# A hybrid decoder layer on one core: group norm's statistics and x's scaling on other engines, attention's causal corner added by TensorE

## The chip, the core and the metric

The kernel runs on one core of one Trainium2 chip. A core has five engines with queues of their own: TensorE (PE; PEld is its weight load), VectorE (DVE), ScalarE (ACT), GpSimd (POOL) and SyncE (SP), which issues most transfers. They meet through semaphores only. The metric is the device time of one execution in microseconds (us). Three runs of the kernel before took 1525.68, 1518.18 and 1522.67 us: median 1522.67. The profile is of one more run.

## The reference, cut to what matters

```
h = RMSNorm(x, pre_norm_g);  proj = h @ w_in          # x: 1024 x 1024
z, xBC, dt, q, k, v, f, z_att, g_ssm, g_att = split(proj)
xs, B, C = split(silu(causal_conv(xBC)))              # 4 groups, state 128
y = chunked SSD scan(xs, dt, B, C), chunks of 128     # 16 heads of 64
yg = y * silu(z);  per group of 256 channels:
yg = yg * rsqrt(mean(yg * yg) + 1e-6) * ssm_norm_g    # "norm" below
s = q.k / 8 + F[t] - F[s], F = cumsum(log_sigmoid(f)) # 16 heads of 64
s = where(kpos <= qpos, s, -inf);  o = softmax(s) @ v
merged = sigmoid(g_ssm) * (yg @ w_b_ssm) + sigmoid(g_att) * ((o * silu(z_att)) @ w_b_att)
out = x + RMSNorm(merged @ w_out, post_norm_g)
```

All is float32. The kernel keeps the precision by splitting an operand into a high part, rounded to the matmul's format (fp32r), and the rest, and by three passes: high x high, high x low, low x high.

## The kernel before

**Stages.** The prologue loads x in eight tiles of 128 rows, scales each row (`norm_tiles`, L766), turns the tiles on TensorE (`turned`, `pt`) and makes the seven operands of a Strassen-like product (`put`). The second four tiles (`hf == 1`) are scaled by GpSimd (L775). Then the big projection runs as a `Stream` of pairs of 128-column strips. A pair has seven steps; a step is two "halves" of six matmuls of 128x512 (`pb`, `pc`, `pd` are their PSUM banks). Weights come into six `raw` buffers, are split (L200, L201) and evicted by ScalarE and VectorE (L246 to L260). Each `half()` also prepares the operand three steps ahead. There are 504 halves in all.

**Work beside the stream.** Everything else is written as generators that `yield n`: `stream.beside` runs n halves of the stream, then goes on. TensorE's matmuls and turns stay in the order in which the program issues them (`mm`, `turn`); a scheduler orders the other engines. Four groups follow one another: pairs up to x's, then the SSD scan `ssd(g)`, then `gate_and_norm(g)` under the next group's pairs. `gate_and_norm` gates y with `z` from DRAM, squares, sums over 256 channels with a matrix of ones (`pv`), and takes the rows of sums to a column tile by DRAM, because a root of one 1x512 row would use one lane: row to `r_dram`, back as `rc` of 128x8 (column b holds rows of block b), root, reciprocal, written to `rr_dram` element by element, and read again as `r`, broadcast to 128 partitions, for the last multiplication (L713). All five transfers are on GpSimd's queue, in order, and each waits for the one before.

**Attention** takes two heads (64 rows each of the array) at a time, eight head pairs. `scores` makes q.k blocks of 128 queries by up to 512 keys (`unit(i, h)`, 12 of them). GpSimd puts a large value into the corner of `fb` above the diagonal (L918, 64 selects of 128x128 in both heads); VectorE adds `fb` to the scores and finds the minimum `nm` (L927); ScalarE takes the exponential and its sum `sm` (L932). `settle` merges the two halves of the keys, `send` turns the 8 columns of maxima (`tp`), copies them to `st`, writes them to `st_dram` and reads them as rows of `nmr[r]`; `send_sums` does the same for the reciprocal sums. `outputs` makes the blocks again, turned (`sT`), with a fourth pass that subtracts the maximum (`nones` x `nmr[h]`), takes the exponential `pt` (L1018), masks its corner on GpSimd (L1023) and multiplies with v (`av`, one block pair later by `flush`). `done` scales `av` with the gate and the reciprocal sum, loaded there (L1042 to L1047). Eight halves of the stream go beside the scores and ten beside the outputs of each head pair; the eighth has four left beside scores and none beside its outputs, where first products with the branch weights (`ps_in`) start.

**After attention** come the branch products, their gates, the output product (`po`) and the last norm; the change leaves them alone.

## Time and profile before

| What | us |
|---|---|
| median of three runs (1518.18 to 1525.68) | 1522.67 |
| the profiled execution, whole | 1512.78 |
| its span, on which the views rest | 1511.0 |
| TensorE busy / VectorE / ScalarE / GpSimd | 1361.1 / 835.9 / 764.8 / 189.8 |
| first block of attention's scores starts | 716.33 |
| one head pair, scores and outputs, mean of the seven with outputs beside the stream | 65.3 |
| scores of the last head pair start | 1173.69 |

The mean granted clock of TensorE in the profiled execution is 0.957 of full speed. The page gives busy time for each engine, a row of tenths in 40 slices of 37.8 us, the chain of work that ended last, and groups of instructions. A group's line reads: source line, engine, operation, out<-in, shape, count, then busy time, mean ns of one, idle time of the engine just before them and what ended it. An engine's idle time is of interest only where TensorE waits as well.

### The profile page before, as it was taken

Reading aid. Unit: us, or ns where it says so; the run is one execution under the profiler, and the core shown is the slowest. Engines: PE = TensorE matmul, PEld = TensorE weight load, DVE = VectorE, ACT = ScalarE, POOL = GpSimd, SP = SyncE. Lnnn points to the kernel's source line nnn. Section 1 sums busy time; section 2 is a strip of 40 time slices with the busy share of each in tenths; the row PEclk is TensorE's granted clock in tenths of the full one; section 3 lists DMA queues with packets and bytes.
Section 4 is the critical chain, followed back from the end, with each engine's and each line's share of the span. In section 5 each row is a group of like instructions: output and inputs, shape, how many; then the busy total and the mean of one; then the engine's idle time right before and its main releaser. Section 6 shows DMA issues by size and latency. Waiting matters only on the chain.

```text
span 1511.0 us, 19901 instructions
## 1 busy us (share of the span) xinstructions
PE 1361.1 (90%) x6866; PEld 1010.4 (67%) x6866; DVE 835.9 (55%) x1671; ACT 764.8 (51%) x1626; POOL 189.8 (13%) x269
## 2 busy tenths in 40 slices
PE   3899999899889988996899888979899779999998
PEld 2577787677667776775565555656565448888786
DVE  5787857776678568765535435152452523444432
ACT  5645556565556555643657467465665731221221
POOL 2000221021103110410010102111021110000000
PEclk8999999999999999998899999989999789999999
DMA  4032332443344324444441424334232635744432
GB/s 179 30 123 61 131 107 74 136 141 125 72 129 148 112 63 140 149 137 133 147 135 69 161 95 158 104 120 146 85 133 92 202 119 188 227 155 149 145 112 84
DMA packets 109925, 189.58 MB, mean 125 GB/s; under 512 B 11168, under 2 KB 36256, under 8 KB 108800
## 3 DMA queue, kind: packets, MB, share of 16 engines
q1 hardware_dynamic: 105840, 179.15, 36.5%
q0 software_dynamic: 2448, 6.87, 1.7%
q10 hardware_dynamic: 1536, 2.29, 0.4%
q8 instruction: 54, 0.88, 0.2%
q14 instruction: 47, 0.39, 0.1%
HBM read 133.45 MB, written 54.82 MB: 125 GB/s over the span
## 4 chain that ended last, share of the span: by engine, by line
PE 61%; DMA 12%; issue 11%; DVE 7%; ACT 5%; POOL 2%; SPq 2%; POOLq 0%; DVEq 0%; ACTq 0%
PE pb L151 17%; PE ps_in L151 12%; PE pc L151 8%; PE po L151 6%; PE sT L151 5%; PE av L151 4%; PE pd L151 4%; DMA th<-st_dram 3%; PE yps L151 2%; DMA raw<-in_wu 2%; DMA csb<-cs_dram 2%; DMA rr_dram<-rc 1%; ACT sf L932 1%; DMA r<-rr_dram 1%; PE s L151 1%
## 5 line engine op out<-in xcount | busy, mean ns | idle before, releaser
L201 DVE TENSOR_TENSOR wop<-sum,wop 128x512 fp32r<-128x512 f32 x144 | 101.2, 705 | 131.1 <-ACT wop L200 130.6
L1018 ACT ACTIVATE pt<-sT,nfcol 128x512 f32<-128x512 f32 (+1 forms) x192 | 96.3, 580 | 92.8 <-PE sT L151 92.8
L932 ACT ACTIVATE sf<-sf,nm 128x512 f32<-128x512 f32 (+1 forms) x192 | 116.4, 608 | 47.0 <-DVE nm L927 43.4
L927 DVE CUSTOM_DVE_ANT_0 sf<-s,fb 128x512 f32<-128x512 f32 (+1 forms) x192 | 99.5, 553 | 48.6 <-POOL fb L918 25.2
L151 PE MATMUL pb<-x5h,wop 128*128 128x512 f32 x288 | 106.1, 422 | 13.8 <-ACT s L246 13.8
L151 PE MATMUL pd<-x1h,wop 128*128 128x512 f32 x288 | 103.9, 413 | 11.8 <-DVE wop L201 11.8
L200 ACT ACTIVATE wop<-sum 128x512 fp32r<-128x512 f32 x144 | 89.7, 623 | 45.9 <-PE pc L151 27.4
L151 PE MATMUL pb<-x6h,wop 128*128 128x512 f32 x288 | 103.7, 412 | 2.8 <-ACT s L246 2.8
L151 PE MATMUL pc<-x3h,wop 128*128 128x512 f32 x288 | 100.0, 401 | 3.2 <-DVE th L260 3.2
L151 PE MATMUL pc<-x2h,wop 128*128 128x512 f32 x288 | 101.8, 406 | 1.2 <-DVE u L258 0.6
L151 PE MATMUL pb<-x0h,wop 128*128 128x512 f32 x288 | 100.4, 400 | 0.0
L151 PE MATMUL pb<-x4h,wop 128*128 128x512 f32 x288 | 99.3, 399 | 0.1
L201 DVE TENSOR_TENSOR wop<-raw,wop 128x512 fp32r<-128x512 f32 x108 | 75.7, 701 | 40.7 <-ACT wop L200 35.9
L151 PE MATMUL av<-pt,v 128*64 128x512 f32 (+3 forms) x384 | 78.2, 520 | 16.7 <-ACT pt L1018 8.5
L246 ACT ACTIVATE s<-pb 128x512 f32<-128x512 f32 x108 | 63.6, 589 | 57.4 <-PE pb L151 57.0
L200 ACT ACTIVATE wop<-raw 128x512 fp32r<-128x512 f32 x108 | 67.1, 622 | 23.7 <-PE pd L151 16.5
L151 PEld LDWEIGHTS pb<-x5h,wop 128*128 128x128 f32 x288 | 57.2, 199 | 31.3 <-ACT s L246 16.4
L151 PEld LDWEIGHTS pd<-x1h,wop 128*128 128x128 f32 x288 | 55.7, 194 | 31.9 <-DVE wop L201 13.1
L151 PEld LDWEIGHTS pb<-x6h,wop 128*128 128x128 f32 x288 | 55.5, 193 | 20.4 <-ACT s L246 5.2
L151 PEld LDWEIGHTS pc<-x3h,wop 128*128 128x128 f32 x288 | 54.4, 189 | 18.5 <-issue 3.4
L151 PEld LDWEIGHTS pc<-x2h,wop 128*128 128x128 f32 x288 | 55.0, 191 | 17.1 <-issue 4.1
L206 DVE TENSOR_TENSOR sum<-raw 128x512 f32<-128x512 f32 x72 | 52.0, 722 | 25.5 <-DMA raw<-in_wu 25.0
(261 smaller groups left out, 3262.7 us busy)
## 6 DMA issues: line engine op xcount, KB each, us to landing
raw<-in_wu SPq DMA_DIRECT2D x128, 256.0 KB
csb<-cs_dram SPq DMA_DIRECT2D x32, 256.0 KB
fb<-f_dram SPq DMA_DIRECT2D x8, 1024.0 KB
raw<-in_wbs SPq DMA_DIRECT2D x9, 512.0 KB
xt<-in_x SPq DMA_DIRECT2D x8, 512.0 KB
zg_dram<-th SPq DMA_DIRECT2D x16, 256.0 KB
qh_dram<-th SPq DMA_DIRECT2D x16, 256.0 KB
ql_dram<-th SPq DMA_DIRECT2D x16, 256.0 KB
```

The costliest lines, as they stand in the source:

```text
L151: return tc.keep_in_program_order(nc.tensor.matmul(*args, **kw))
L200: nc.scalar.activation(op[:, 0], src, AF.Copy)
L201: nc.vector.tensor_tensor(op[:, 1], src, op[:, 0], ALU.subtract)
L206: nc.vector.tensor_tensor(t, x, y, ALU.add)
L246: nc.scalar.activation(s, ps, AF.Copy)
L927: nc.vector.tensor_tensor_reduce(sf[:, e, 0:w], s[e][:, 0:w], fb[:, e, c0:c1], 1.0, 3.0e38, ALU.add, ALU.min, nm[h][:, e, i : i + 1],)
L932: nc.scalar.activation(sf[:, e, 0:w], sf[:, e, 0:w], AF.Exp, scale=-1.0, bias=nm[h][:, e, i : i + 1], accum_out=sm[h][:, e, i : i + 1],)
L1018: nc.scalar.activation(pt[:, e, 0:w], s[e][:, 0:w], AF.Exp, scale=-1.0, bias=nfcol[:, b, 2 * hp + e : 2 * hp + e + 1],)
```

## The change

TensorE's program grows from 6336 to 6876 instructions: 256 matmuls and as many weight loads for the corner of the scores in bfloat16 (`eye` x `far`, 64 rows), 36 small turns of the norm, and 8 turns fewer in attention. GpSimd's list shrinks from 269 to 179: 64 selects, 4 scalings and 24 transfers go, 2 of setup come. SP issues 12 more transfers.

- **x:** ScalarE scales the second four tiles; the squares' scratch moves to the `th` ring.
- **Norm:** the row of sums is copied to `line`, four turns a half bring it into columns (`pv_t`, `rc`); after root and reciprocal one turn (`pr`) gives eight rows, written with 512 bytes a row and read as `r`, on SP. `z` is loaded two halves ahead into the `csb` ring. L713's successor is kept in program order.
- **Pairs:** z, (b, c), q, x, k, v in a group; the norm no longer waits for the v pair, and the turn of v comes after three halves.
- **Corner:** two passes per head on the diagonal 128 columns add the large value above the diagonal, for the scores alone; the `pt` corner stays on GpSimd.
- **Maxima and sums:** one `nmr` tile holds both halves' rows, `pick[h]` selects; maxima of the upper half are turned a yield later; those of the lower half and the reciprocal sums are turned together (24 columns, `ns`), beside the outputs' second pair of blocks. The gate is loaded and multiplied ahead (`gates`).
- **Halves:** ten before attention instead of eight; five among the score blocks and three after the last (before: seven and one), six beside the outputs; 26 halves in all move ahead of attention. The first branch weights load in another order.

```diff
@@ -678,40 +678,54 @@
             sl = half(ch)
             sq = []
             for j in range(2):
-                z = small()
+                z = sp.tile([P, 4, P], F32, tag="csb", bufs=2, name="z").rearrange("p a b -> p (a b)")
                 nc.sync.dma_start(z, zg_dram[2 * g + j, :, sl])
+                sq.append(z)
+            yield 2
+            for j in range(2):
+                z = sq[j]
                 nc.vector.tensor_tensor(xs[j][:, sl], xs[j][:, sl], z, ALU.mult)
                 nc.scalar.activation(z, xs[j][:, sl], AF.Square)
-                sq.append(z)
             nc.vector.tensor_tensor(sq[0], sq[0], sq[1], ALU.add)
...
             yield 6
             pv = pp.tile([P, HALF], F32, tag="tr", bufs=2, name="pv")
             for j in range(2):
                 mm(pv, onesr, sqp[j], start=(j == 0), stop=(j == 1))
-            row = sp.tile([P, 4, P], F32, tag="ce", bufs=1, name="row").rearrange("p a b -> p (a b)")[0:1, :]
-            nc.scalar.activation(row, pv[0:1, :], AF.Identity, bias=eps4[0:1, :], scale=1.0 / 256.0)
-            nc.gpsimd.dma_start(r_dram[g : g + 1, sl], row)
-        rc = sp.tile([P, NT], F32, tag="rc", bufs=1, name="rc")
-        nc.gpsimd.dma_start(rc, r_dram[g].rearrange("(b p) -> p b", p=P))
-        yield 5
-        nc.scalar.activation(rc, rc, AF.Sqrt)
+            line = sp.tile([P, 4, P], F32, tag="ce", bufs=1, name="line")[0:1]
+            nc.scalar.activation(line, pv[0:1, :].rearrange("p (a b) -> p a b", a=4), AF.Copy)
+            yield 2
+            pc = pp.tile([P, HALF], F32, tag="tr", bufs=2, name="pv_t")
+            for b in range(4):
+                turn(pc[:, b : b + 1], line[:, b, :], ident[0:1, 0:1])
+            if ch == 0:
+                rc = sp.tile([P, NT], F32, tag="rc", bufs=1, name="rc")
+            nc.vector.tensor_copy(rc[:, 4 * ch : 4 * ch + 4], pc[:, 0:4])
+        nc.scalar.activation(rc, rc, AF.Sqrt, bias=eps4, scale=1.0 / 256.0)
         nc.vector.reciprocal(rc, rc)
-        nc.gpsimd.dma_start(rr_dram[g].rearrange("(b p) -> p b", p=P), rc)
+        yield 3
+        pr = pp.tile([P, HALF], F32, tag="tr", bufs=2, name="pr")
+        turn(pr[0:NT, 0:P], rc)
+        row = sp.tile([P, 4, P], F32, tag="ce", bufs=1, name="row")[0:NT, 0, :]
+        nc.scalar.activation(row, pr[0:NT, 0:P], AF.Copy)
+        nc.sync.dma_start(rr_dram[g].rearrange("(b p) -> b p", p=P), row)
         r = [sp.tile([P, 4, P], F32, tag="csb", bufs=2, name="r").rearrange("p a b -> p (a b)") for _ in range(2)]
         for ch in range(2):
-            nc.gpsimd.dma_start(r[ch], rr_dram[g : g + 1, half(ch)].to_broadcast([P, HALF]))
+            nc.sync.dma_start(r[ch], rr_dram[g : g + 1, half(ch)].to_broadcast([P, HALF]))
         yield 5
         for ch in range(2):
...
+                tc.keep_in_program_order(
+                    nc.vector.scalar_tensor_tensor(
+                        xs[j][:, sl], xs[j][:, sl], ng[:, i : i + 1], r[ch], ALU.mult, ALU.mult
+                    )
                 )
                 nc.sync.dma_start(ys_dram[i, :, sl], xs[j][:, sl])
...
     def groups_pairs(g):
         return [
+            both("z", g, lambda i: silu_gate(zg_dram, i)),
             Pair((("b", g), ("c", g)), (conv(g, "bt", 8 + g), conv(g, "ct", 12 + g))),
-            both("z", g, lambda i: silu_gate(zg_dram, i)),
+            both("q", g, lambda i: parts(qh_dram, ql_dram, i, -0.125)),
             Pair((("x", 2 * g), ("x", 2 * g + 1)), tuple(conv(g, f"xs{j}", 2 * g + j) for j in range(2))),
-            both("q", g, lambda i: parts(qh_dram, ql_dram, i, -0.125)),
             both("k", g, lambda i: parts(kh_dram, kl_dram, i, 1.0)),
             both("v", g, values),
         ]
...
-    order[0:4] = [order[n] for n in (1, 3, 0, 2)]
+    order[0:4] = [order[n] for n in (0, 2, 1, 3)]
...
-                sqt = wp.tile([P, HALF], F32, tag="s", bufs=3, name="sqt").bitcast(BF16)
+                sqt = small("sqt").bitcast(BF16)
                 nc.scalar.activation(sqt, xt, AF.Square, accum_out=ss[:, t : t + 1])
...
                 if hf == 0:
                     nc.vector.tensor_scalar(xt, xt, rstd[:, t : t + 1], None, ALU.mult)
                 else:
-                    nc.gpsimd.tensor_scalar(xt, xt, rstd[:, t : t + 1], None, ALU.mult)
+                    nc.scalar.activation(xt, xt, AF.Copy, scale=rstd[:, t : t + 1])
...
             stream.beside(norm)
-            stream.until(by_group[g][2])
+            stream.until(by_group[g][3])
             stream.halves(7)
             stream.beside(ssd(g))
-            stream.until(order[6] if g == 0 else by_group[g][5])
             norm = gate_and_norm(g)
...
+        nmr = ap.tile([P, HALF], F32R, name="nmr")
+        pick = [ap.tile([P, 1], F32R, name=f"pick{h}") for h in range(2)]
+        eye = ap.tile([P, 192], BF16, name="eye")
+        far = ap.tile([P, 192], BF16, name="far")
+        nc.vector.memset(eye, 0.0)
+        for t in (nmr, *pick):
+            nc.vector.memset(t.bitcast(F32), 0.0)
+        big, beyond = small("big"), small("beyond")
+        nc.vector.memset(big[:, 0:192], -NEG)
+        for e in range(2):
+            for h in range(2):
+                nc.vector.memset(pick[h][64 * e + 32 * h : 64 * e + 32 * h + 1, :].bitcast(F32), -1.0)
+            nc.vector.tensor_copy(eye[rows[e], 64:P], ident[rows[e], rows[e]])
+            nc.gpsimd.affine_select(
+                beyond[:, 192 * e : 192 * e + 192], big[:, 0:192], [[1, 192]], ALU.is_gt, 0.0, base=64 * e - 64,
+                channel_multiplier=-1,
+            )
+            nc.vector.tensor_copy(far[rows[e], :], beyond[rows[e], 192 * e : 192 * e + 192])
+        corner = [(eye[:, 64:192], far[:, 64:192]), (eye[:, 0:P], far[:, 0:P])]
...
+        def to_rows(cols, n):
             tp = pp.tile([P, HALF], F32, tag="s", bufs=4, name="tp")
             turn(tp[0:n, 0:P], cols)
-            st = ap.tile([16, P], F32, tag="st", bufs=2, name="st")
+            st = ap.tile([24, P], F32, tag="st", bufs=1, name="st")
             nc.scalar.activation(st[0:n, :], tp[0:n, 0:P], AF.Copy)
...
+            return st
...
+        def keep_maxima(hp, r, st):
+            nc.sync.dma_start(st_dram[hp, 0:2, half(r)].rearrange("e (i p) -> e i p", p=P), st)
+        def send_maxima(hp, r):
+            for e in range(2):
+                row = nmr[64 * e + 32 * r : 64 * e + 32 * r + 1, :]
+                nc.sync.dma_start(row.bitcast(F32), st_dram[hp, e : e + 1, half(r)])
...
+        def passes(s, w, ops, corner_at=None):
+            for m, (x, y) in enumerate(ops):
+                for e in range(2):
+                    mm(
+                        s[e][:, 0:w], x[rows[e]], y[rows[e]], start=(m == 0),
+                        stop=(m == len(ops) - 1 and corner_at is None), skip_group_check=True,
+                    )
+            if corner_at is not None:
+                for n, (x, y) in enumerate(corner):
+                    for e in range(2):
+                        mm(
+                            s[e][:, corner_at : corner_at + P], x[rows[e]], y[rows[e]], start=False, stop=(n == 1),
+                            skip_group_check=True,
+                        )
+        def blocks(name):
+            return [pp.tile([P, HALF], F32, tag="s", bufs=4, name=name) for e in range(2)]
...
+            nr1 = ap.tile([P, 2, 4], F32R, tag="nr1", bufs=2, name="nr1")
+            ns = ap.tile([P, 24], F32R, tag="ns", bufs=2, name="ns")
+            nr = [ns[:, 0:8].rearrange("p (e i) -> p e i", e=2), nr1]
+            inv = ns[:, 8:24].rearrange("p (e i) -> p e i", e=2)
...
-                if h == i // 4:
-                    gsl = slice(i * P, (i + 1) * P)
-                    nc.gpsimd.affine_select(
-                        fb[:, :, gsl], fb[:, :, gsl], [[0, 2], [-1, P]], ALU.is_ge, -NEG, base=0, channel_multiplier=1
-                    )
...
+                s = blocks("s")
+                ops = [(q[x][:, isl], k[y][:, 0:w]) for x, y in (("qh", "kh"), ("qh", "kl"), ("ql", "kh"))]
+                passes(s, w, ops, w - P if h == i // 4 else None)
...
+            def finish():
                 nc.vector.tensor_scalar(sm[0], sm[0], 2.0, None, ALU.mult)
-                nc.vector.reciprocal(sm[0], sm[0])
...
+                nc.vector.reciprocal(inv.bitcast(F32), sm[0])
+            def send():
+                st = to_rows(ns.bitcast(F32), 24)
+                keep_maxima(hp, 0, st[0:8, :])
+                nc.sync.dma_start(st_dram[hp, 2:4, :].rearrange("e (i p) -> e i p", p=P), st[8:24, :])
...
             unit(7, 0)
             unit(6, 0)
-            yield 2
+            yield 1
             unit(5, 0)
             unit(4, 0)
             settle(1)
-            yield 2
+            yield 1
             unit(3, 0)
             unit(2, 0)
-            send(1)
             yield 1
+            keep_maxima(hp, 1, to_rows(nr1.bitcast(F32).rearrange("p e i -> p (e i)"), 8)[0:8, :])
+            send_maxima(hp, 1)
             unit(1, 0)
             unit(0, 0)
             settle(0)
-            sums()
-            waiting.append(lambda: send(0))
-            yield 1
-            flush()
-            waiting.append(send_sums)
+            finish()
+            sends.append(send)
+            yield 3
+        sends = []
         def outputs(hp, qk, v, more):
+            zr = {}
+            def gates(h):
+                sl = half(h)
+                zr[h] = ap.tile([P, HALF], F32, tag="zr", bufs=1, name="zr")
+                nc.sync.dma_start(zr[h], za_dram[hp, :, sl])
+                rb = small()
+                for e in range(2):
+                    nc.sync.dma_start(rb[rows[e], :], st_dram[hp, 2 + e : 3 + e, sl].to_broadcast([64, HALF]))
+                nc.gpsimd.tensor_tensor(zr[h], zr[h], rb, ALU.mult)
...
+                    s = blocks("sT")
+                    ops = [(k[x][:, bsl], q[y][:, o:]) for x, y in (("kh", "qh"), ("kl", "qh"), ("kh", "ql"))]
+                    passes(s, w, ops + [(pick[h].to_broadcast([P, P]), nmr[:, o:])])
...
                 def done(h=h, av=av):
-                    sl = half(h)
...
-                for b in range(0, last + 1, 2):
+                    with tc.high_priority():
+                        nc.vector.tensor_tensor(zr[h], av[0], zr[h], ALU.mult)
+                    nc.sync.dma_start(ya_dram[hp, :, half(h)], zr[h])
+                for n, b in enumerate(range(0, last + 1, 2)):
                     flush()
+                    if (h, n) == (1, 1):
+                        sends.pop()()
                     waiting.append(unit(b))
                     waiting.append(unit(b + 1))
+                    if (h, n) in ((1, 2), (0, 0)):
+                        gates(h)
                     if b + 2 > last:
                         waiting.append(done)
                         more(h)
-                    yield 1 if b < 4 * h else 2
+                        if h:
+                            send_maxima(hp, 0)
+                    yield (1, 1, 0, 2)[n] if h else 1
...
-        stream.halves(8)
+        stream.halves(10)
...
-            ws = [load_split(a["wbs"][i], [P, NK, P]) for i in range(2)]
...
+        ws = [load_split(a["wbs"][0], [P, NK, P])]
+        next(go)
+        ws.append(load_split(a["wbs"][1], [P, NK, P]))
         products = first_products()
         for n, _ in enumerate(outputs(hp, [qk[hp, 0], qk[hp, 1]], v, more)):
-            for _ in range((3, 1, 1, 1, 1, 1)[n]):
+            for _ in range((2, 1, 1, 1, 1, 1)[n]):
                 next(go, None)
-            if n:
+            if n > 1:
                 next(products)
```

## The prediction

> **What bounds the kernel now.** I read the page first, then TensorE's waits, then windows of 25 us, and last the timelines of the places where a window is thin.
>
> ```profile
> span 1511.0 us, 19901 instructions
> ...
> PE 1361.1 (90%) x6866; PEld 1010.4 (67%) x6866; DVE 835.9 (55%) x1671; ACT 764.8 (51%) x1626; POOL 189.8 (13%) x269
> ...
> PE   3899999899889988996899888979899779999998
> ...
> PEclk8999999999999999998899999989999789999999
> ...
> PE 61%; DMA 12%; issue 11%; DVE 7%; ACT 5%; POOL 2%; SPq 2%; POOLq 0%; DVEq 0%; ACTq 0%
> ```
>
> TensorE is busy 90% of the span and no other engine over 55%. So time can come only from the 150 us in which it is idle, and from stretches in which its clock digit is under 9. The waits say who leaves it idle (total us, times, longest):
>
> ```profile
> PE tp L154 <- DVE sm L965: 19.7, 8, 3.1
> PE pb L151 <- ACT s L246: 16.6, 9, 6.9
> PE pt L154 <- POOL xt L775: 14.5, 4, 7.5
> PE s L151 <- DVE nm L927: 12.7, 25, 3.4
> PE pd L151 <- DVE wop L201: 11.8, 3, 5.6
> ...
> PE tp L154 <- DVE nm L927: 9.0, 8, 1.7
> ...
> PE tp L154 <- DVE nr L944: 7.8, 8, 3.3
> ```
>
> The three `tp` lines (36.5 us) are attention's turned sums and maxima, `pt` the second half of x, `pb` and `pd` weights or evictions late behind the group norm. The windows (length, PE, PEld, DVE, ACT and POOL busy, granted clock, DMA share, GB/s) place them:
>
> ```profile
> 25.00:50.00 25.00, 10.95 (x44) 5.44 (x45) 11.90 (x23) 12.40 (x24) 11.67 (x4) 0.66 0.10 32
> ...
> 250.00:275.00 25.00, 19.41 (x79) 15.46 (x78) 14.38 (x26) 10.35 (x21) 2.02 (x3) 0.86 0.40 112
> ...
> 700.00:725.00 25.00, 12.60 (x36) 7.99 (x34) 11.11 (x20) 4.05 (x8) 1.52 (x3) 0.73 0.78 269
> ...
> 1175.00:1200.00 25.00, 17.60 (x96) 11.36 (x94) 17.96 (x63) 21.38 (x61) 5.08 (x8) 0.81 0.57 190
> 1200.00:1225.00 25.00, 14.57 (x56) 7.71 (x58) 10.08 (x10) 12.04 (x18) 3.33 (x2) 0.70 0.65 201
> ```
>
> A thin window also has a granted clock under 1.00: a wait is paid for again in slow matmuls after it (12 matmuls of 512 columns, a step of the stream, take 2.75 us at full clock). The norm's chain shows among the transfers (KB, median us from issue to landing):
>
> ```profile
> r<-rr_dram POOLq DMA_DIRECT2D x8, 256.0 KB, 4.2
> ...
> r_dram<-row POOLq DMA_DIRECT2D x8, 2.0 KB, 1.8
> ...
> rc<-r_dram POOLq DMA_DIRECT2D x4, 4.0 KB, 3.5
> rr_dram<-rc POOLq DMA_DIRECT2D x4, 4.0 KB, 10.2
> ```
>
> Writing 4 KB as 1024 pieces of 4 bytes takes 10.2 us.
>
> **Part 1, ScalarE scales x.** GpSimd scales four tiles in 11.67 us (28.74 to 40.4, 2.9 each); TensorE waits 7.46 + 3 x 2.35 = 14.5 us for them. A 128x1024 pass takes ScalarE 1.05 us, so four cost 4.2. `sqt` also moves to another ring, and the instruction order now puts the squares ahead of and between the first operands' copies, where ScalarE idles some 8 us between 10.9 and 25; x has landed by then. ScalarE's last operand copy before the second half's rows ends at 27.5 now; without its squares and roots (4 x 1.5) and with four scalings it would end at 29 at most, against 40.5. I take -11; if the scalings queue behind everything, 4.5 is added to 27.5 and -8 is left; with the slow clock (0.66) gone too, -13.
>
> **Part 2, norm at three inner boundaries.** At group 0, the row goes out at 242.85, `rc` comes back, the write of `rr_dram` runs 250.3 to 260.3, `r` lands at 265.2; VectorE idles 8.36 us for it, with the next weight split behind it on its queue, and TensorE 5.59 (then 1.43 and 1.31). Against the typical pace of the stream the three boundaries lose 6.5, 8.3 and 9.0 = 24 us. Now the columns come by eight turns, the root is taken on 128x8, one turn gives eight rows of 512 bytes: `r_dram` and `rc` go, the write has the 1.7 us of attention's `st_dram` write, the read stays at 4.2 to 4.9. From the reciprocal: 3 halves (4.1 us), the turn, 0.3 copy, 1.7 + 4.9 us, with 5 halves (6.9 us) of cover: VectorE comes to `xs` about when `r` lands. The write, and both reads, move from GpSimd's queue to SP's, where they wait for ScalarE's `row` ahead of later weight loads; those have six buffers, so a wait under one step costs nothing, and over it, itself. Added on TensorE: 9 small turns a group, 0.5 us, 2 in all. I leave 4 us of stalls: -18 (bounds -10, the write and its waits late; -24, all gone).
>
> That the reads join the loads is weighed by one more rule. The Trainium skill, "DMA: Bandwidth & Descriptors", section "Issuing engines are not separate DMA queues", says that transfers from all issuing engines end on the same 16 DMA engines. By it the read gains nothing from the other queue; the sum has nothing for it either.
>
> The pairs' new order, `z` loaded two halves before its use (into `csb`), and `v` turned a half later move work under the same stream and add no operation: 0. Their cover is the stream; without it a 256 KB load is 4.2 us per half group.
>
> **Part 3, last boundary and attention's start.** There TensorE idles 6.86 at 707.83 (weights late behind the scattered write) and 3.21 at 716.33 (first `qh`), and runs at half clock until 744. From `pv` at 684.2 to the first score 14 halves (19.4 us) take 32.1: 12.7 lost. The first scores phase takes 35.66 against 22.3 for the same work without a gap or slow clock: 13.4 lost, with VectorE waiting 8.25 for GpSimd's mask on `fb`, whose load was issued at 715.46. Now ten halves instead of eight stand between loads and scores, the mask is gone, and the write is short. Of 26 us I take 15 (bounds 8 and 22): the load of `fb` (1 MB) still shares the stretch with `r`.
>
> **Part 4, attention.** Head pairs 1 to 6 take 64.7 us; clean, scores are 22.3 (8 halves) and outputs 32.5 (10). Above that the phases lose 39 (scores 1 to 6), 21 (outputs 0 to 6), 12 (last scores) and 17 (last outputs and what follows): 89. Four halves per head pair move ahead of attention: the same 5.5 us elsewhere, 0, but cover that is gone here. Terms after:
>
> - corner on TensorE: 64 diagonal blocks x 2 passes x 2 heads = 256 matmuls of 128 columns. Eight such take 0.42 us in the 128-wide score blocks (pairs of heads side by side), with weight loads of 64x128 (0.185 each) hidden: 0.105 a pair, 13. No bf16 pair is in the trace; bounds 7 (half of the row of 256 columns, 0.11) and 256 x 0.185 = 47, every load exposed. I take 13, since the nearest row hides the same loads.
>
> The Trainium skill speaks against the corner: "TensorE: Matmul & The Clock Gate", section "LDWEIGHTS (loading the stationary operand)", says a load costs by its 128 columns, however few rows it has (107 ns by its formula). By that the corner would be an estimated 27 us and the sum 14 worse; the 128-wide score blocks already run faster than it.
>
> - new waits: the turned maxima are now sent behind a half and the sums with row 0 in one turn, three halves after the last block, which takes out the `tp` waits. In return the units (7,0) and (5,0) have one half behind them instead of two, `av` of blocks 4 and 5 follows its `sT` with no half between (exp 0.52 + select + latency, about 1.5), row 0 of `nmr` is read on SP behind four 256 KB loads of the next `qk` (1.5 past two halves), row 1 0.5, scores 1.5: about 5 per head pair with slow clock, 40 in all (bounds 16 and 76).
> - the tail: the split of `ys` starts only after the last half; ten 512 KB loads through two buffers take about 5.8 us a pair, under outputs with 12 score blocks as cover: 20 lost against 17 + 12 before's last phases (bounds 10 and 30).
>
> 13 + 40 + 20 = 73 against 89: -16. With every bound together -50 and +64; with two of three at their bad ends, +20 to +35.
>
> **The sum.** -11 - 18 - 15 - 16 = -60. The profiled run took 1512.8 (span 1511.0), so 1452.8; the median shown is 9.9 above it, and I predict in its terms: 1463.
>
> **Rivals.**
> 1. Attention's waits only change places. For it: outputs already waits 8.2 for `th` L1047 and 8.5 for `pt`; against: 36.5 us of `tp` waits have no successor of their size. Attention +8 instead of -16, boundaries -6 instead of -18: -24, 1499.
> 2. More comes out: few new waits (attention -40 and each other term near its good end): -90, 1433. For it: boundary losses repeat at each group with one cause.
> 3. Slower: ScalarE and VectorE pace the scores when the cover is thin. Place: blocks (7,0) to (0,0). The last head pair, with four halves, shows it: 28.5 us for work of 16.8, ScalarE busy 21.38 of 25, VectorE 17.96, TensorE 17.60. At that pace plus one half (1.4), then three halves (4.1) and the corner (1.6), scores take 35.6 against 28.8 on average: +6.8, x 8 = 54. Outputs keep their loss. -11 - 18 - 5 + 54 = +20: 1543. It decides from +4.3 us per scores phase (34 / 8), above 33. Against: 25.2 us of VectorE's idle time ahead of those blocks was GpSimd's masks.
> 4. Corner's weight loads exposed: 47 instead of 13: -26, 1497. That the norm's chain isn't shortened would need the 512-byte write to cost as the 4-byte one: +18, 1481, inside the range.
>
> **How the numbers follow.** Forecast 0.50 (own range 1440 to 1485), rival 1 0.18, rival 2 0.15, rival 3 0.12, rival 4 0.05. A change below 0.5% (7.6 us) can't be told from none here. Rivals 1 and 4 reach into "same" with a fifth of their chance; rival 3 is slower with 0.10 and same with 0.02: faster 0.84, same 0.06, slower 0.10. Leaving out the far ends of rivals 2 and 3, the range is 1425 to 1510.
>
> **What would show it.** Right: POOL gone from `pt`'s releasers and window 25:50 above 18 busy; no idle VectorE over 3 us before `xs`; `tp` waits under 10 us; no slow clock in 725:750. Wrong: `rr_dram` or `nmr` landing after 5 us; scores phases over 33 us; `av` or `sT` waiting for `pt` or `nmr` more than 2 us each head pair; corner matmuls spaced over 0.15 us a pair.

## The result and the profile after

The changed kernel takes 1420.72 us (median of four runs, 1416.50 to 1424.67) against 1520.70 (four runs, 1518.18 to 1525.68): 6.6% faster, ratio 0.9338 with a 95% interval of 0.9300 to 0.9377. That is 100 us, where 60 were forecast; the time lies 4 us below the range of 1425 to 1510. The direction and the kind of gain were right, the sizes too small.

The page of the changed kernel (busy time, tenths in 40 slices of 35.4 us, granted clock in tenths, chain of waits):

```profile
span 1414.8 us, 20283 instructions
...
PE 1343.9 (95%) x7150; PEld 1002.7 (71%) x7150; DVE 830.1 (59%) x1689; ACT 763.5 (54%) x1626; POOL 133.7 (9%) x179
...
PE   6899999999999999999999999999999799999998
...
PEclk9999999999999999999999999999999999999999
...
PE 75%; ACT 9%; DMA 7%; DVE 5%; issue 2%; SPq 1%; POOL 0%; DVEq 0%; ACTq 0%; POOLq 0%
```

TensorE is busy 95% of the span, and no slice has a clock digit under 9; the mean granted clock went from 0.957 to 0.991. In the clock's record, stretches at half speed add up to 131.3 us before and 27.0 after. DMA's share of the chain fell from 12% to 7%, GpSimd's from 2% to 0.

TensorE's waits after (us in total, times, longest):

```profile
PE av L151 <- POOL pt L1074: 14.9, 9, 3.0
PE pb L151 <- ACT s L246: 12.5, 9, 2.7
...
PE s L151 <- ACT st L921: 5.5, 8, 1.2
PE s L151 <- DVE nm L979: 3.2, 4, 2.3
PE av L151 <- ACT pt L1069: 3.1, 2, 2.1
...
PE sT L151 <- DMA nmr<-st_dram: 1.4, 4, 0.5
```

The three `tp` waits (36.5 us) are gone, as are GpSimd's four for `pt` in the prologue (14.5) and `pd` behind the norm (11.8). New are `av` behind GpSimd's mask on the probabilities, 5.5 us for the copy `st`, and little for `nmr` (1.4). The windows at the old thin places (length, busy PE, PEld, DVE, ACT, POOL, granted clock, DMA share, GB/s):

```profile
25.00:50.00 25.00, 22.97 (x103) 11.93 (x101) 23.53 (x39) 18.61 (x31) 0.00 (x0) 1.00 0.13 43
...
250.00:275.00 25.00, 22.40 (x91) 17.74 (x91) 21.72 (x35) 15.68 (x31) 1.27 (x1) 0.93 0.50 140
...
700.00:725.00 25.00, 21.76 (x131) 14.40 (x129) 17.11 (x54) 17.30 (x47) 0.00 (x0) 0.93 0.49 184
...
1125.00:1150.00 25.00, 20.55 (x104) 14.15 (x104) 9.27 (x8) 12.47 (x21) 4.79 (x8) 0.80 0.62 204
```

The prologue's window went from 10.95 to 22.97 busy. The window that still has a clock of 0.80 is the start of the branch products beside the last outputs.

Where the 96 us of the two profiled executions (1511.0 and 1414.8) come from can be read by milestones: the start of a certain matmul in both traces, with the stream's halves issued until then counted at 1.375 us each, so that halves moved across a milestone cancel. ("Saved" is the difference so corrected, "step" its growth from one milestone to the next.)

| Milestone on TensorE | before (halves) | after (halves) | saved | step |
|---|---|---|---|---|
| first `df` (prologue) | 41.72 (4) | 27.74 (4) | 14.0 | 14.0 |
| first scan, group 0 | 163.27 (69) | 150.29 (69) | 13.0 | -1.0 |
| first scan, group 1 | 309.46 (153) | 309.80 (167) | 18.9 | 5.9 |
| first scan, group 2 | 459.18 (237) | 449.63 (251) | 28.8 | 9.9 |
| first scan, group 3 | 609.33 (321) | 591.34 (335) | 37.2 | 8.4 |
| first score | 716.33 (374) | 702.80 (400) | 49.3 | 12.0 |
| first `ps_in` (end of attention) | 1213.39 (504) | 1120.88 (504) | 92.5 | 43.2 |
| end | 1504.09 (504) | 1408.04 (504) | 96.0 | 3.5 |

### The profile page after: what moved, and what is told of

Read it like the earlier page. It is cut to its first block, busy times and chain, and to the rows that moved or that the text cites. A ratio compares the mean times of both kernels' runs of the same rounds, so it can differ in the third digit from the quotient of the medians.

```text
span 1414.8 us, 20283 instructions
## 1 busy us (share of the span) xinstructions
PE 1343.9 (95%) x7150; PEld 1002.7 (71%) x7150; DVE 830.1 (59%) x1689; ACT 763.5 (54%) x1626; POOL 133.7 (9%) x179
## 4 chain that ended last, share of the span: by engine, by line
PE 75%; ACT 9%; DMA 7%; DVE 5%; issue 2%; SPq 1%; POOL 0%; DVEq 0%; ACTq 0%; POOLq 0%
PE pb L151 21%; PE ps_in L151 12%; PE pc L151 12%; PE po L151 6%; PE pd L151 6%; PE sT L151 5%; PE av L151 4%; ACT sf L984 4%; DMA csb<-cs_dram 2%; PE yps L151 2%; PE s L151 1%; DVE sf L979 1%; DMA nmr<-st_dram 1%; PE st L151 1%; ACT wop L200 1%
## 5 line engine op out<-in xcount | busy, mean ns | idle before, releaser
L979 DVE CUSTOM_DVE_ANT_0 sf<-s,fb 128x512 f32<-128x512 f32 (+1 forms) x192 | 97.2, 553 | 28.7 <-PE s L151 9.8
L620 POOL TENSOR_TENSOR ce<-ce,ct 128x512 f32<-128x512 f32 x28 | 37.9, 1352 | 368.0 <-ACT ce L619 245.2
L607 ACT ACTIVATE m<-csb,cscol 128x128 f32<-128x128 f32 x128 | 41.3, 391 | 48.0 <-DMA csb<-cs_dram 25.1
```

The lines of the kernel that those rows point to most:

```text
L607: nc.scalar.activation(m4[:, h, :], csb[:, h, :], AF.Relu, scale=-1.0, bias=cscol[:, c, 4 * g + h : 4 * g + h + 1])
L620: nc.gpsimd.tensor_tensor(ce, ce, ct[:, cs].unsqueeze(1).to_broadcast([P, 4, P]), ALU.mult)
L979: nc.vector.tensor_tensor_reduce(sf[:, e, 0:w], s[e][:, 0:w], fb[:, e, c0:c1], 1.0, 3.0e38, ALU.add, ALU.min, nm[h][:, e, i : i + 1],)
```

## The experiments

Each of the first ten undoes one part of the changed kernel, or two, or doubles one. "Slower" is against the changed kernel's median, 1420.7; the kernel before took 1517.8 to 1519.5 us beside these sets, 1520.7 beside the changed kernel. The runs of one kernel spread over 3 to 13 us (8 for the changed kernel), so differences of 2 or 3 us can't be told from none. The parts, undone, add up to most of the gain: the squares' ring 14.5, the norm's way 38, mask and sends together 36, of 100.

**x by GpSimd again.**

```diff
-                    nc.scalar.activation(xt, xt, AF.Copy, scale=rstd[:, t : t + 1])
+                    nc.gpsimd.tensor_scalar(xt, xt, rstd[:, t : t + 1], None, ALU.mult)
```

> The changed kernel with one line undone: GpSimd scales the second four tiles of x again; the squares keep their new ring. The prologue gained 13 us. Theory 1, the engine that scales is the cause: GpSimd's 11.7 us for four tiles stand alone again and the kernel is about 13 us slower than the changed one (1434). Theory 2, the squares' new ring is half of it, since the roots are ready some 10 us earlier and GpSimd starts at about 19 instead of 28.7: only 4 to 6 us slower (1426).

1425.95 (1424.83 to 1430.94), 5 us slower, which is theory 2 by the time; but the first `df` comes at 28.48, only 0.7 us later, and the rest is not placed. So the other half was tried by itself.

**The squares back in the old ring.**

```diff
-                sqt = small("sqt").bitcast(BF16)
+                sqt = wp.tile([P, HALF], F32, tag="s", bufs=3, name="sqt").bitcast(BF16)
```

> The changed kernel with ScalarE scaling x but the squares' scratch back in the ring of three that the stream's evictions use. With GpSimd scaling and the new ring the first df came only 0.7 us later. Theory 1, the ring is what moved the squares ahead: the first df comes 6 to 10 us later than in the changed kernel (at 34 to 38 instead of 27.7) and the kernel is 6 to 10 us slower. Theory 2, either of the two alone suffices: under 2 us.

1435.18 (1433.61 to 1436.88), 14.5 us slower, first `df` at 37.17 (9.4 later): theory 1 by the place, 4.5 us beyond it by the time. ScalarE's timeline of this kernel, the first square of the second four tiles (start, us, instruction):

```profile
25.29 1.05 ACT L783 ACTIVATE sqt<-xt 128x1024 bf16<-128x1024 f32 x1
```

and of the changed kernel, the first and last square of the second four tiles:

```profile
11.45 1.06 ACT L783 ACTIVATE sqt<-xt 128x1024 bf16<-128x1024 f32 x1 [0.47 <-DMA xt<-in_x]
...
17.70 1.04 ACT L783 ACTIVATE sqt<-xt 128x1024 bf16<-128x1024 f32 x1
```

The squares' scratch shared three buffers with the stream's evictions and so stood behind them in turn; in the other ring the squares run 14 us earlier. With the new ring GpSimd's 11.9 us of scaling start at 13.4 instead of 28.7 and fit under the first halves too. The scaling by ScalarE, which the change names, gives 4.6 us of the prologue's 14 where the ring is old (41.72 to 37.17), and 0.7 where it is new.

**The norm by DRAM, all of it, and the scattered write alone.** First the old chain (row to `r_dram`, `rc`, root, `rr_dram`, on GpSimd's queue; its lines stand in the diff above), then only its write:

```diff
-        pr = pp.tile([P, HALF], F32, tag="tr", bufs=2, name="pr")
-        turn(pr[0:NT, 0:P], rc)
-        row = sp.tile([P, 4, P], F32, tag="ce", bufs=1, name="row")[0:NT, 0, :]
-        nc.scalar.activation(row, pr[0:NT, 0:P], AF.Copy)
-        nc.sync.dma_start(rr_dram[g].rearrange("(b p) -> b p", p=P), row)
+        nc.sync.dma_start(rr_dram[g].rearrange("(b p) -> p b", p=P), rc)
```

> The changed kernel with the norm's old way through DRAM (r_dram, rc, rr_dram element by element, all on GpSimd's queue); pair order, early z and the removed stop before the norm stay. From the first scan to the first score the change gained 36 us. Theory 1, the chain of five transfers is the cause: 25 to 36 us slower than the changed kernel (1446 to 1457). Theory 2, the pairs' new order and the missing stop give the cover: at most 10 us slower (1430).

> The changed kernel in which the reciprocals go to DRAM straight from the column tile, in pieces of 4 bytes, on SP; the turn of the rows, its copy and the 512-byte write go. The first step of the chain (columns by turns) stays. The old chain cost 42 us over the four boundaries. Theory 1, the scattered write is most of it, 10 us against under 2: 6 to 9 us at each boundary, 25 to 35 slower (1446 to 1456). Theory 2, the number of transfers on one queue is: 1 to 3 us a boundary, under 12 slower.

The whole chain: 1458.65 (1456.45 to 1460.46), 38 us slower, 9.3, 11.2, 10.9 and 12.3 at the four boundaries. The write alone: 1456.72 (1455.09 to 1459.41), 36 us slower, with 5.8, 10.1, 8.7 and 9.2 there. Theory 1 in both, 1 to 2 us beyond its range. SP's queue at the first boundary of the kernel with the scattered write, and of the changed kernel:

```profile
242.21 0.38 SPq L712 DMA_DIRECT2D rr_dram<-rc  x1
251.40 3.13 SPq L715 DMA_DIRECT2D r<-rr_dram  x2
```

```profile
243.49 0.34 SPq L716 DMA_DIRECT2D rr_dram<-row  x1
244.71 0.82 SPq L719 DMA_DIRECT2D r<-rr_dram  x2
```

The read goes out when the write has landed: 9.2 us after it in pieces of 4 bytes, 1.2 us in rows of 512 (9.1 to 12.4 and 1.2 to 1.3 over the four boundaries). The scattered write costs the same on SP's queue as the whole old chain on GpSimd's, so it is not the queue. One turn on TensorE is worth nearly all of the norm's part; the first step (columns by turns instead of `r_dram` and `rc`) adds 2 us, inside the scatter.

**The old pair order and stop.** (z second, q fourth, `stream.until` the v pair before the norm.)

> The changed kernel with the old order of a group's pairs and the old stop, by which the norm waits until the v pair is through. Theory 1, order and stop move work alone: within 4 us. Theory 2, they give the norm's chain another pair's steps to run under, so that its end meets the convolutions of the next group: 8 to 15 us slower over the four boundaries.

1418.11 (1415.34 to 1419.28): 3 us faster, not told from none. Theory 1; by itself the reordering is worth nothing that these runs can tell.

**The mask, the sends, and both.** The mask back on GpSimd (`affine_select` on `fb`, no corner), then the sends and the scores' cover at their old places, then both:

```diff
             unit(6, 0)
-            yield 1
+            yield 2
...
-            yield 1
+            yield 2
             unit(3, 0)
             unit(2, 0)
-            yield 1
             keep_maxima(hp, 1, to_rows(nr1.bitcast(F32).rearrange("p e i -> p (e i)"), 8)[0:8, :])
             send_maxima(hp, 1)
+            yield 1
...
-            sends.append(send)
-            yield 3
...
+            waiting.append(send)
+            yield 1
+            flush()
...
```

> The changed kernel with the corner undone: GpSimd writes the large values into fb again, TensorE adds no corner. Theory 1, the masks made the waits of attention and the corner is a good trade: 13 us of TensorE come back and 20 to 35 us of waits return, so 5 to 20 us slower (1426 to 1440). Theory 2, attention gained by the later sends alone: the corner is pure cost and the kernel is 10 to 13 us faster (1409).

> The changed kernel with the old places of the sends and of the cover in the scores: maxima of the upper half turned right after blocks (3,0) and (2,0), sums and the other maxima one half after the last block, and the halves among the blocks 1, 1, 2, 2, 0, 1 and 1 at the end. Theory 1, the later sends are what attention gained: TensorE waits again for the turned sums, 2 to 3 us and more in each head pair with the slow clock behind it, 20 to 30 us slower than the changed kernel (1441 to 1451). Theory 2, GpSimd's masks were the root of those waits: without them VectorE is on time, at most 6 us slower, and perhaps faster, since two halves again cover the blocks (7,0) to (4,0).

> The changed kernel with both the mask back on GpSimd and the sends at their old places. Alone the mask cost 12 us by the runs and the early sends 11. Theory 1, the two add up: 20 to 26 us slower than the changed kernel (1441 to 1447). Theory 2, they make one chain (mask, VectorE's minimum, reciprocal, turn), whose idle time is long enough to halve the clock behind it: 33 to 45 us slower (1454 to 1466), with over 40 us of slow clock in attention, as before the change.

1433.54 (1428.27 to 1434.32), 13 slower; 1431.95 (1431.26 to 1436.24), 11 slower; both 1457.16 (1456.09 to 1458.95), 36 slower. The mask alone is theory 1, the sends alone lie between their theories, and both together cost 12 more than their sum: theory 2 of the third run, with 47.8 us at half clock between the first score and the first `ps_in`. TensorE's timeline at the turn of the sums, head pair 2 (start, us, instruction, idle before), with both, and with the early sends alone:

```profile
859.39 0.28 PE L154 MATMUL tp<-ident,ns 128*24 128x128 f32 x1 [3.41 <-DVE ns L1012]
```

```profile
847.11 0.27 PE L154 MATMUL tp<-ident,ns 128*24 128x128 f32 x1 [1.29 <-DVE ns L1007]
```

and windows of the kernel with both, around it:

```profile
850.00:860.00 10.00, 5.15 (x30) 3.55 (x32) 7.16 (x27) 6.77 (x22) 1.61 (x3) 1.00 0.58 205
860.00:866.00 6.00, 6.00 (x28) 3.61 (x26) 0.00 (x0) 2.53 (x4) 0.73 (x2) 0.72 0.24 74
```

VectorE, late by GpSimd's masks, is late with the reciprocal: TensorE waits 3.41 us instead of 1.29, and behind that the clock falls (0.72 in the window after it). With both, each of the first seven outputs phases has 3.41 us at half clock; with either alone none of them has any. The longer wait itself makes up the excess, though: a scores phase (head pairs 1 to 5) takes 27.5 us with both, 25.3 with the early sends alone, 24.3 with the mask alone and 24.5 with neither. The outputs phases (head pairs 1 to 6) take 30.6 with both, slow clock included, and 30.8 with the mask alone, where `sT` waits up to 1.6 us for `nmr`. TensorE's wait of 3.41 us has the length of a stretch of slow clock by chance: the seventh such wait was 2.88 us and had 3.41 at half clock behind it too.

**The corner twice.**

```diff
-                for n, (x, y) in enumerate(corner):
+                for n, (x, y) in enumerate(corner + corner):
...
```

> The changed kernel with the corner's two passes made twice (512 matmuls instead of 256; the masked value is doubled). Theory 1, a pair of corner matmuls takes 0.105 us as in the 128-wide score blocks: 13 us slower (1434). Theory 2, each weight load of 128 columns counts: 27 us (0.107 each) to 47 us (0.185 each) slower. Theory 3, it fills waits of TensorE for VectorE: under 6 us slower.

1425.21 (1423.86 to 1430.25), 4.5 us slower; a scores phase grows from 24.5 to 24.74. The timeline of the changed kernel's TensorE, a block's corner and the next block:

```profile
815.38 0.29 PE L151 MATMUL s<-far,eye 64*128 64x128 bf16 x4
815.48 0.42 PE L151 MATMUL s<-kh,qh 64*128 64x384 f32 x2
```

Four corner matmuls take 0.10 us from start to the next start, and where they are doubled four more take 0.11: 0.05 to 0.06 a pair, half of the value taken, 6.4 to 7.2 us for the 128 pairs. The kernel with the mask on GpSimd agrees: there TensorE's scores phase, less its idle time, is 0.79 us shorter, 6.3 in eight. Doubling hides partly in waits (idle time of a scores phase 0.77 to 0.57). Theory 3 holds by its time.

**The gate late.** (`gates(h)` at the head of `done` again.)

> The changed kernel with the gate and the reciprocal sums loaded and multiplied at the end of each outputs phase again, not ahead. Theory 1, the next phase's first av waits for that product again as before (8.2 us in 4 waits): 8 to 15 us slower (1429 to 1436). Theory 2, the early sums are enough and the loads land under the last blocks: within 4 us.

1422.75 (1422.28 to 1428.44), 2 us slower: theory 2.

**Tries at a faster kernel.** The cover of the upper half's outputs spread evenly, then with its empty place at blocks without a mask:

```diff
-                    yield (1, 1, 0, 2)[n] if h else 1
+                    yield 1
```

```diff
-                    yield (1, 1, 0, 2)[n] if h else 1
+                    yield (1, 0, 1, 2)[n] if h else 1
```

> A try at a faster kernel: in the outputs of the upper half one half of the stream after each two blocks (1, 1, 1, 1) in place of 1, 1, 0, 2. In the changed kernel av waits 14.9 us for the masked pt, 1.25 to 3.0 a time, where no half lies between. Theory 1, that wait goes and nothing takes its place: 6 to 9 us faster than the changed kernel (1412 to 1415). Theory 2, row 0 of the maxima then lands late for the next sT (two halves lay over its read): the wait moves there, within 3 us.

> The changed kernel with the cover in the upper half's outputs as 1, 0, 1, 2: the two blocks without a half behind them are (2) and (3), whose pt has no mask, and the two halves over the read of row 0 stay. Even cover (1, 1, 1, 1) had been 19 us slower. Theory 1, that loss was the read of the maxima (two halves are needed there) and av's wait is for GpSimd's mask: 5 to 9 us faster than the changed kernel (1412 to 1416). Theory 2, av waits for ScalarE's exponential as long as for the mask, or GpSimd's product of the gate comes to lie before the mask: within 3 us, or up to 10 slower.

1439.33 (1436.77 to 1450.11), 19 us slower, and 1420.90 (1415.49 to 1424.57), the same. Waits of the first:

```profile
PE av L151 <- POOL pt L1074: 14.2, 8, 3.1
...
PE sT L151 <- DMA nmr<-st_dram: 11.4, 7, 2.0
```

and of the second:

```profile
PE av L151 <- POOL pt L1074: 6.3, 3, 2.4
...
PE sT L151 <- DMA nmr<-st_dram: 3.5, 5, 1.4
```

Evenly spread, the wait for row 0 of the maxima grows from 1.4 to 11.4 us while the mask's stays: theory 2, but six times its price. Slow clock makes up most of the rest. The seven outputs phases beside the stream are 16.5 us longer in all; TensorE is idle in them 8.5 us more, and four of them have about 3.4 us at half clock, where the changed kernel has none. The clock changes only on a grid of 3.41 us, and what counts is how much idle time falls into one window of it. Windows of the even cover's kernel around two waits for row 0, of 1.66 us (ended at 817.03) and of 1.67 us (ended at 872.58):

```profile
814.17:817.59 3.42, 1.76 (x17) 1.11 (x15) 1.98 (x3) 0.66 (x2) 0.00 (x0) 1.00 0.91 301
817.59:821.00 3.41, 3.41 (x14) 2.58 (x11) 0.00 (x0) 2.21 (x4) 0.81 (x2) 0.50 0.27 77
868.79:872.20 3.41, 2.12 (x16) 0.97 (x14) 1.98 (x3) 1.11 (x2) 0.41 (x1) 1.00 0.90 303
872.20:875.61 3.41, 3.03 (x18) 2.23 (x20) 0.00 (x0) 2.21 (x4) 0.41 (x1) 1.00 0.38 133
```

The first wait lies in one window, and the next window has half clock; the second is cut in two (1.29 and 0.38 us), and nothing follows. The last section has the count over all traces.

In the second try (theory 2) the mask's wait falls by 8.6 us, and the time stays: idle time of the seven outputs phases fell from 1.3 to 2.3 each to 0 to 1.7 (6 us in all), but the phases are less than 1 us shorter in all. Why is not shown.

Then `r` in the ring `th`, alone, with the old pairs, and with the moved cover:

```diff
-        r = [sp.tile([P, 4, P], F32, tag="csb", bufs=2, name="r").rearrange("p a b -> p (a b)") for _ in range(2)]
+        r = [small("r") for _ in range(2)]
```

> A try at a faster kernel: the two broadcast tiles r of the norm go to the ring th instead of csb. In the changed kernel the next scan's first csb load waits for r to be used, ScalarE stands at it, and TensorE waits 12.5 us for evictions behind that. Theory 1, the ring is that wait: 5 to 8 us faster (1413 to 1416). Theory 2, th (four buffers) is short then and the stream's own results wait for it: 0 to 10 us slower.

> A try at a faster kernel: old pair order and stop (1418.1 alone) with r in the ring th (1419.0 alone). Theory 1, the two small gains are real and add up: 3 to 6 us faster than the changed kernel (1415 to 1418). Theory 2, both are scatter between runs: within 3 us.

> All three of the above together. Theory 1: 10 to 14 us faster than the changed kernel (1407 to 1411). Theory 2: no faster than the changed kernel.

1418.99 (1411.13 to 1423.67) alone, not told from none; 1411.74 (1409.83 to 1414.33) with the old pairs, 9 us faster and beyond theory 1; 1414.21 (1410.23 to 1416.38) with all three, 6.5 us faster, between its theories. In the middle one each of the six runs lies under the changed kernel's four; its ratio to the kernel before is 0.9311 (0.9277 to 0.9344), whose interval overlaps the changed kernel's, and the kernel before was 3 us faster beside it. Its wait for evictions shows where the gain may come from:

```profile
PE pb L151 <- ACT s L246: 2.4, 4, 0.7
```

It was 12.5 in the changed kernel: there the next scan's `csb` load waits until `r` is used, ScalarE waits for `csb`, and evictions stand behind it. With the ring alone it is 4.4, with the old pairs alone 9.0. So the ring takes most of this wait, and the 3.41 us of slow clock behind it at two boundaries; why its time falls only with the old pairs was not tried.

## Why the prediction came out as it did

| Term | forecast | measured | by |
|---|---|---|---|
| prologue | -11 | -13.0 | milestones |
| three inner boundaries | -18 | -24.3 | milestones |
| last boundary and first scores | -15 | -12.0 - 7.3 = -19.3 | milestones; first scores 35.66 to 28.35 |
| attention and tail | -16 | -43.2 + 7.3 - 3.5 = -39.4 | milestones, less the first scores |
| pair order | 0 | 0 | old order, 3 us faster |

**The step that failed is the size of the attention term's new waits**: "about 5 per head pair with slow clock, 40 in all". Counted as the prediction counts, by how far the phases lie above their clean lengths, they cost 25: the scores of head pairs 1 to 6 lie 13.3 above, outputs 0 to 6 with six halves 16.6, less 4.8 for the corner. The mechanism (late sends remove the `tp` waits, others come in return) was right; three of the four waits hardly came. `av` behind `pt`, put at 1.5 a head pair, is 1.2 to 2.2 in the first seven, as said (9.7 of its 18.0; the rest falls after the last outputs start). But rows 0 and 1 of `nmr`, put at 1.5 and 0.5, cost 1.4 in all, and the blocks (7,0) and (5,0), put at 1.5, wait for VectorE in the first scores phase alone (3.2). `st`, 0.6 a phase, wasn't foreseen. Idle time in these 13 phases is 15.8 us; the other 9 are not placed.

The four waits add up to 5.0 a head pair by themselves, so the words "with slow clock" had no figure in the sum. Slow clock did not come either: from the wait before the first score to the first `ps_in` half speed takes 71.7 us before and only 3.4 after, in the first scores phase; idle time falls from 62.8 to 23.9. The new waits are short and lie apart, so that no window of 3.41 us in those 13 phases has more than 1.95 us of idle time. With mask and early sends back, 3.41 us of waiting puts 2.4 to 3.0 into one window, and half clock follows each time.

The Trainium skill, "TensorE: Matmul & The Clock Gate", section "What's actually happening", says that the clock falls to half after an idle window of about 3.4 us and comes back after a busy one. The traces agree with the window's length, but not with a whole window of idle time: a wait of 1.66 us was enough once in the even cover, and each window with over 1.95 us idle was followed by half clock.

The corner was put at 13 and takes 6.4 to 7.2, at the lower of its bounds. The tail, put at 20 with the last scores, was right: the last scores lie 1.7 above their clean length, and from the start of the last outputs to the end the kernel takes 303.0 us, before 301.9, as lossy as it was (17). Together that is 25 + 4.8 + 1.7 + 18 = 50 us lost instead of 73.

Two sums of that part are off: with every term at its lower bound 7 + 16 + 10 = 33 against 89 is -56, not -50, and two of three at their bad ends give +28 to +54, not +20 to +35. The result lies inside the terms' own bounds (-13 - 24 - 22 - 56 = -115); the range ended above it because the far end of the second rival was left out.

**Boundaries.** Right in cause, to the piece: the 4-byte write was 9.2 of the chain. I left 4 us of stalls at three boundaries, and took 1.7 for the short write, which took 1.2; VectorE has no wait before `xs` at the first boundary. The three boundaries gave the far end of the bounds, 24. At the last one two things were mixed: 12.0 came before the first score, most of it by the write, as the scattered write's run shows (9.2 back there). The first scores' 7.3 came from attention's changes: that phase takes 35.3 us again with mask and early sends both back, 29.5 with either, 29.4 with the scattered write. TensorE did not run at half clock until 744 there either; the slow clock came in three stretches, the last ended at 733, and the granted clock is 0.99 from there to 744.

**Prologue.** The size was near, the credit wrong: the text put the scaling first and the ring second, and the runs show the ring first. ScalarE's idle time between 10.9 and 25 was 6.9 us, not 8.

**Rivals.** Of the rivals, the second ("more comes out", 1433) describes what came: attention -39.4, three inner boundaries and prologue at their good ends. It was priced 12 us short. The third, by which thin cover lets ScalarE pace the scores, did not happen: a scores phase takes 24.5 us, far from the 33 from which it decides, and the last one 21.3 with six halves. The even cover shows that thin cover can decide all the same, in another place: the read of the maxima, with the slow clock behind it.

## What to carry to other kernels

Look first for transfers of single elements in a chain that others wait for, and turn on TensorE instead: here one turn of 128x8 was worth 36 us. Two delays on one chain can cost far more together (36 us) than apart (13 and 11), so undo them in pairs before a part is credited. When you price a new wait, ask also how much idle time it puts into one 3.41 us window of the clock. Scratch in a shared ring is a wait that no source line shows: ask in whose turn a buffer comes free.

## What the runs showed of the hardware

**The clock.** In the 17 traces here the granted clock is 1.00 or 0.50 and changes only at whole multiples of 3.413 us from its first change. From 100 us on, without the last 15, they hold 6361 such windows at full clock. Of the 94 in which TensorE was idle over 1.95 us, all were followed by half clock; of the 60 with 1.6 to 1.95, 22; of the 6207 with less, 11, which stay unexplained. So a wait of about half a window can halve the clock, and whether it does hangs on where the grid cuts it. (Ends of matmuls are modelled, so these limits are rough.)

**The corner.** Corner matmuls in bf16 with 64 rows go in 0.05 to 0.06 us a pair of heads (128 columns), half of the fp32 pairs of the 128-wide score blocks (0.105), with a weight load of half the length (changed kernel, groups by line, mean ns after the busy time):

```profile
L151 PE MATMUL s<-far,eye 64*128 64x128 bf16 x256 | 20.8, 222 | 0.0
L151 PEld LDWEIGHTS <-eye 64*128 64x128 bf16 x256 | 9.8, 95 | 7.2 <-issue 6.7
```

The fp32 load of the same 64x128 takes 185 to 206 ns. The Trainium skill's rule, in "LDWEIGHTS (loading the stationary operand)" of "TensorE: Matmul & The Clock Gate", which the forecast weighed against the corner, gives 107 ns for 128 columns by its formula. That is near the bf16 load's 95 and half of the fp32 one's, and it doesn't give the pace: the 256 bf16 loads add up to 24.3 us and have a busy time of 9.8, so loads run at the same time, and the corner's matmuls start 0.025 us apart on average.
